# Layer 0's first stage: single k tiles, three a_u heads, and an order of three engines written out

## The chip, the cores and the metric

The kernel runs on one core of a Trainium2 chip. The metric is the device time of one execution in microseconds (us). Engines are named as in the profile: PE (TensorE), with PEld for its weight loads, DVE (VectorE), ACT (ScalarE), POOL (GpSimd) and SP (SyncE, which only issues DMAs here; its queue is SPq).

## The reference

Two trunk layers work on a latent stream x (256 x 2048) and a context stream ctx (256 x 2048), in float32. What matters for the change is the start of layer 0:

```python
shift, scale, gate = split(silu(c) @ w_mod[l] + b_mod[l], 3)
h   = rmsnorm(x, g_pre[l]) * (1 + scale) + shift          # the same for ctx with c_ctx
proj = h @ w_in[l]
a_u, a_v, a_g, b_q, b_k, b_v, b_g, c_x, c_g = split_cols(proj)
y_a = chunk_gmlp(gelu(a_u), gelu(a_v), ...) * silu(a_g)   # a_u, a_v: 512 columns, 4 heads of 128
...
x = x + gate * rmsnorm(concat(y_a, y_b, y_c) @ w_out[l], g_post[l])
```

So nothing of layer 0 can be multiplied before shift and scale of at least one slice of 128 features are known, and they need columns of w_mod (2048 x 6144 per layer), and 1/rms of every token, which needs all of x.

## The kernel before

**Tiling.** The 2048 features are 16 k tiles of 128 (KT). Both streams lie side by side, feature-major, as 16 tiles yo0..yo15 of 128 x 512 (256 latent and 256 context tokens). Every product with w_in is done as three passes (mm3, L383): hi x hi, hi x lo, lo x hi, with each operand cut exactly into two float32r parts. h becomes hh and hl per k tile (make_h, L445: two DVE operations, two ACT casts and two DVE operations of 128 x 256). Weights come as halves of 128 x 1024 (512 KB) into one of three raw buffers; ACT casts whi (L367) and DVE subtracts wlo (L368). Stream (L329) hands them out in a fixed order.

**The first stage of layer 0** (layer, L496) runs over k outermost and keeps six sums in PSUM, four of a_v (128 tokens x 512 columns each) and two of a_u (heads 0 and 1, "au01"). For each k it does 12 products of a_v (start_av) and 6 of a_u (start_au). The two other a_u heads follow as units of their own (tunit, L473: one head of 128 columns, 16 k tiles x 3 passes = 48 products), then c_x, a_g, c_g, k, v, q, b_g, and the output projection.

**The modulation** of k tiles k0.. (mod_start, L154) is computed inside this stage on PE: silu(c) (cpad, 32 columns wide) against scale and shift columns of w_mod, in four groups kg of four k slices. DVE transposes the sum (L177), eight tiny products gather it (ps_modc, L182), and DVE adds biases to get gs and sh (L191 to L194, "the columns"). It comes by pairs of k tiles for k 0 to 7 (PAIRS; 4 MB of w_mod per pair, 16 DMAs of 256 KB into the hh8..hl15 tiles) and by single tiles for k 8 to 15 (ALONE; 2 MB per tile, into two sets of buffers taken in turn). mod_start is a generator: the loop over blocks steps the next block's products between the a_v and a_u products of this one.

**Order.** PE's order is the program's (manual_schedule). The other engines' orders are found by the tile framework, which orders instructions by priority and by their data. The remaining modulation (gate of layer 0, all of layer 1; mod_rest, L265) runs on DVE as multiply-adds of 128 x 512 (L209), so many steps per weight half by RATE and pace (L287). Later (L296) hands other engines' products back to PE after delays counted in PE time; branch_a yields such delays before the mixing products (ps_mix). NEAR (L279) says how many weight halves ahead of the one in use are requested at the start.

**Buffers.** PSUM has six "mm" banks (the sums of products) and two "ms" banks for small things (ps_mod, ps_modc, ps_rs, ps_rb, ps_mix). w2k is a ring of seven 2 KB-per-partition tiles.

**The start** (L989 to L1014): the small loads, x in 16 DMAs, sums of squares (ACT L467, DVE L468), first modulation block, 1/rms (col_sums, POOL pow, bcast as ps_rb), two weight halves, then layer(0).

Of the kernel before, what the change touches and what calls it, by code (L numbers as in the profile page):

```python
# [23 lines left out]
PAIRS, ALONE = [0, 2, 4, 6], list(range(8, KT))  # L24
# [3 lines left out]
def units():  # L28
    """(name, first column, columns, first k tile, k tiles): blocks of w_in of 128 x 2048 each."""
    u = []  # L30
    u += [("av", COL["av"], 512, 4 * i, 4) for i in range(4)]
    u += [("au01", COL["au"], 256, 8 * i, 8) for i in range(2)]
    u += [(f"au{h}", COL["au"] + 128 * h, 128, 0, 16) for h in (2, 3)]
    u += [(f"cx{h}", COL["cx"] + 128 * h, 128, 0, 16) for h in range(4)]
    u += [(f"ag{h}", COL["ag"] + 128 * h, 128, 0, 16) for h in range(4)]
    u += [(f"cg{h}", COL["cg"] + 128 * h, 128, 0, 16) for h in range(4)]
    u += [(f"k{h}", COL["k"] + 128 * h, 128, 0, 16) for h in range(2)]
    u += [("v", COL["v"], 256, 8 * i, 8) for i in range(2)]
    u += [(f"q{h}", COL["q"] + 128 * h, 128, 0, 16) for h in range(8)]
    u += [(f"bg{h}", COL["bg"] + 128 * h, 128, 0, 16) for h in range(8)]  # L40
    return u
# [25 lines left out]
def trunk_kernel(ctx: ExitStack, tc: tile.TileContext, xT, xhalf, cT, wss, wsl, wmod, win, wout0, wout1, const, vec, rows,  # L67
# [24 lines left out]
    # ---- constants  # L92
    ct = sb([P, KT, 2], F32, "ct")
    DMA.dma_start(ct, cT)
    vecs = sb([P, 2, NVEC], F32, "vecs")
    DMA.dma_start(vecs, vec)
# [8 lines left out]
    A.activation(cs, ct, AF.Silu)  # L105
    cpad = sb([P, KT, 32], F32, "kt0")
    V.memset(cpad, 0.0)
    V.tensor_copy(cpad[:, :, 0:2], cs)

    class low:  # L110
        """instructions that may wait for the next `n`."""
# [22 lines left out]
    # ---- modulation: columns [128, 16, stream] of scale, shift and gate  # L134
# [5 lines left out]
    def mod_cols(l, cb, ps8):  # L140
        """ps8 [128, 4, 2]: silu(c) @ w_mod for 512 columns of column block cb."""
        what, j0 = cb // 4, (cb % 4) * 4
        b = vc(l, "bmod")[:, cb * 4:cb * 4 + 4].unsqueeze(2).to_broadcast([P, 4, 2])
        sl = slice(j0, j0 + 4)
        if what == 0:
            V.tensor_tensor(out=sh[l][:, sl], in0=ps8, in1=b, op=ALU.add)
        else:
            dst = (gs[l] if what == 1 else gg0)[:, sl]
            g = vc(l, "gpre" if what == 1 else "gpost")[:, sl].unsqueeze(2).to_broadcast([P, 4, 2])
            V.scalar_tensor_tensor(out=dst, in0=ps8, scalar=1.0 if what == 1 else 0.0, in1=b,  # L150
                                   op0=ALU.add, op1=ALU.add)
            V.tensor_tensor(out=dst, in0=dst, in1=g, op=ALU.mult)

    def mod_start(k0, nk):  # L154
        """scale and shift of k tiles k0 .. k0 + nk - 1 of layer 0 on the tensor engine: yields after
        each unit's products, and before the columns."""
        ps = ms_ps("mod")
        n = 2 * P * nk
        for kg in range(4):
            src = wss[PAIRS.index(k0), kg] if nk == 2 else wsl[ALONE.index(k0), kg]  # L160
            if nk == 1:
                tags = (("mraw", "mraw", "macc", "vv"), ("mg", "mgl", "yo0 yo1", "yo2 yo3"))[k0 % 2][kg]
            else:
                tags = " ".join(f"{t}{8 + 2 * kg + i}" for i in range(2) for t in ("hh", "hl"))
# [31 lines left out]
    def mod_dve(l, cb, red):  # L196
        """red [128, 2, 16]: sums over the 32 partitions of each quadrant, transposed."""
# [38 lines left out]
    def mod_gate1():  # L236
        """products of silu(c) and the gate's columns of w_mod in layer 1, still to be summed over partitions."""
# [16 lines left out]
    def gate1():  # L254
        """(sum + b_mod) * g_post of layer 1's gate, on all partitions."""
        for c in range(4):
            r = sb([P, 2, 512], F32, "mraw", 2)
            DMA.dma_start(r, rows[None, :, c * 512:(c + 1) * 512].to_broadcast([P, 2, 512]))
            ps = ms_ps("gate")
            PE.matmul(ps, ones, g1[c], start=True, stop=True)  # L260
            V.tensor_tensor(out=g1[c], in0=r[:, 0], in1=ps, op=ALU.add)
            V.tensor_tensor(out=g1[c], in0=g1[c], in1=r[:, 1], op=ALU.mult)
            yield YT
# [13 lines left out]
    RATE = dict(au0=2, cx0=2.2, ag0=2.2, cg0=2.2, k0=2, v0=2, q0=1.8, bg0=2.2, out0=2.8,  # L277
                k1=2.5, v1=2.5, q1=1, bg1=2.2)
    NEAR = [1] * 6 + [0] * 6 + [1, 2, 3]  # L279
# [7 lines left out]
    def pace():  # L287
        """steps of the modulation due per half of a unit, behind the latest weights on the vector engine."""
# [6 lines left out]
    # ---- work of other engines that hands products back to the tensor engine later  # L295
    class Later:  # L296
# [19 lines left out]
        def flush(self):  # L316
# [8 lines left out]
            (("yo8 yo9", 1), ("yo10 yo11", 1)), (("yo12 yo13", 1), ("yo14 yo15", 1))]  # L325
    BACK = 8

    # ---- weights: raw -> exact parts hi + lo, in halves of a unit, ahead of their use
    class Stream:  # L329
        AHEAD = 3  # L330

        def __init__(self):
            self.src, self.out, self.pos, self.stop = [], [], 0, 0
            self.place, self.behind = {}, {}
            for l in range(2):
                def half(name, i, h):
                    return win[l, UIDX[name][i], h]
                for i in range(2):
                    self.src += [half("av", 2 * i, 0), half("au01", i, 0), half("av", 2 * i, 1),
                                 half("av", 2 * i + 1, 0), half("au01", i, 1), half("av", 2 * i + 1, 1)]  # L340
                for i, u in enumerate(UNITS):
                    if u[0] not in ("av", "au01"):
                        self.src += [win[l, i, 0], win[l, i, 1]]
# [10 lines left out]

        def emit(self):
            tags = self.place.get(len(self.out), (("whi", NHI), ("wlo", NLO)))
            r = sb([P, 1024], F32, "raw", NRAW)
            DMA.dma_start(r, self.src[len(self.out)])
# [29 lines left out]
    def part(w, c):  # L388
        """columns c of both parts; a part is a tile or a list of tiles side by side."""
# [19 lines left out]
    # ---- per-token reciprocal rms from sums over features  # L409
# [14 lines left out]
    def col_sums(ps, q, n, start=True, stop=True):  # L424
        """columns of ps: sums over the partitions of q [128, n * 128], one accumulation group."""
# [10 lines left out]
    # ---- streams in feature-major tiles  # L436
    yo = [None] * KT
# [7 lines left out]
    def make_h(l, k, rb, streams):  # L445
        """h = x * rstd * gs + sh, as hi + lo; rb: rstd over the tokens of `streams`."""
# [26 lines left out]
    def tunit(n, sl=None):  # L473
        """feature-major product of one unit of 128 columns: PSUM [128, n]."""
# [18 lines left out]
    blocks = [(k, 2) for k in PAIRS] + [(k, 1) for k in ALONE]  # L493

    # ---- one layer, up to the inputs of the output projection
    def layer(l):  # L496
# [12 lines left out]
        # a_v (token-major) and two heads of a_u, k outermost  # L509
        av = [mm_ps("av") for _ in range(nt)]  # L510
        au = [mm_ps("au") for _ in range(2)]
# [6 lines left out]
        def start_au(k):  # L518
            for j in range(2):
                c = slice((k % 4) * 256 + j * P, (k % 4) * 256 + (j + 1) * P)  # L520
                mm3(au[j][:, 0:n], part(auw, c), (hh[k][:, 0:n], hl[k][:, 0:n]), k == 0, k == KT - 1)
            later.tick(PASS * 512 * nt + PASS * n * 2)

        for i, (k0, nk) in enumerate(blocks):
            mod = mod_start(*blocks[i + 1]) if l == 0 and i + 1 < len(blocks) else iter(())

            def step():
                next(mod, None)

            for k in range(k0, k0 + nk):  # L530
                made = prep_h(l, k)
            if l == 1 and i == 0:
# [7 lines left out]
            for _ in range(2 if nk == 2 else 4):  # L540
                step()
            start_av(k0, range(nt))
            if nk == 2:
                start_au(k0)
                step()
                step()
                start_av(k0 + 1, range(nt // 2))
            step()
            if nk == 2:
                start_av(k0 + 1, range(nt // 2, nt))  # L550
# [28 lines left out]
        # branch A  # L579
        def branch_a():  # L580
            vt = [w2k([P, 512]) for _ in range(nt)]
            ss = sb([P, 4], F32, "ss")
            for j in range(2):
# [8 lines left out]
            yield 12.0 if l == 0 else 7.0  # L592
            for h in range(4):
# [9 lines left out]
                yield (12.0 if h == 1 else 2.0) if l == 0 else (7.0 if h == 1 else 2.0)  # L603

        # branch C
# [9 lines left out]
        def fourier(g, ps):  # L615
            """cos(2 pi t m / 256) is even in t around 128 and sin odd: positions t and 256 - t are added for the one
            and subtracted for the other, which leaves 128 rows each (position 128 in the sines' row of t = 0)."""
# [25 lines left out]
        # branch B  # L643
        def rope(hi, lo, ps):
            """x * cos + rot(x) * sin of the latents, and x of the context, as hi + lo."""
# [97 lines left out]
        for h in (2, 3):  # L743
# [56 lines left out]
    # ---- output projection  # L800
# [33 lines left out]
    def finish():  # L834
        """layer 1's output projection with tokens on partitions, and x1 + gate * y / rms(y)."""
        x1 = {}

        def turn():
            """x1 of the latents to tokens on partitions: [128, token tile, 512] per 512 columns."""
# [68 lines left out]
    def boundary(s, acc):  # L908
        """x1 = x0 + gate * y / rms(y) of stream s in place, and its own 1 / rms."""
# [50 lines left out]
    def prep_h(l, k):  # L960
        new_h(k)
        if l == 0:
            return make_h(0, k, rb0, [0, 1])
        return make_h(1, k, rbs[0], [0])

# [23 lines left out]
    with tc.manual_schedule(engines={mybir.EngineType.PE}):  # L989
        # ---- start: modulation of the first k tiles, x and its statistics  # L990
        raw = w2k([P, NFIRST])
        DMA.dma_start(raw, const[:, 0:NFIRST])
        A.copy(identr, raw[:, 0:P])
        A.copy(cst[:, 0:NFIRST - P], raw[:, P:])
        for k in range(KT):
            yo[k] = sb([P, T], F32, f"yo{k}")
            DMA.dma_start(yo[k], xT[k])
# [3 lines left out]
        m = mod_start(*blocks[0])  # L1001
# [3 lines left out]
        dg = rstd_diag(ps[:, 0:4], 4, D)  # L1005
# [4 lines left out]
        next(m)  # L1010
        W.emit()
        W.emit()
        list(m)
# [81 lines left out]
```

## Time and profile before

| what | value |
|---|---|
| median of 3 runs | 1171.07 us (1170.23 to 1173.67) |
| profiled execution: span from the first to the last instruction | 1167.9 us |
| mean granted TensorE clock | 0.996 |
| PE matmul groups of units (ps_t, L384 to L386) | 1346.5 us of records, which overlap, 3888 products |
| HBM read | 231.08 MB, 200 GB/s over the span |
| DMA, 10 to 120 us | 338 to 398 GB/s |
| first a_v product / last of the stage | 37.30 us / 136.4 us |
| DVE after the stage, waiting before wlo at 141.67 | 5.64 us |

The profiled execution's own device time isn't listed apart from its span; the median of the runs is 3.2 us above the span. A row of the timeline or of the chain begins with its start and its length in us; matmul records overlap, since they are pipelined, so the distance between starts (0.23 us for a product of 512 columns) is the cost of one.

### The profile page before, as it was taken

The numbers are of one execution on the slowest core, as the hardware profiler recorded it, in microseconds if no ns is written. First come the engines' busy times: TensorE is split into PE (matmuls) and PEld (weight loads), VectorE is DVE, ScalarE is ACT, GpSimd is POOL, SyncE is SP. The second block draws the span as 40 slices with busy tenths as digits, with TensorE's granted clock in tenths as the row PEclk, the third lists the DMA queues.
The fourth block names the chain that finished last, engine by engine and source line by source line (L and its number), as shares of the span: only waits on it lengthen the run. The fifth ranks groups of instructions, "written<-read, shape, count | busy, mean of one in ns | idle before, by whom it ended". The sixth has DMA issues, their size and how long they took to land.

```text
span 1167.9 us, 17483 instructions
## 1 busy us (share of the span) xinstructions
PE 1136.0 (97%) x6656; PEld 953.7 (82%) x6656; DVE 881.8 (76%) x1469; ACT 509.8 (44%) x914; POOL 17.3 (1%) x23
## 2 busy tenths in 40 slices
PE   3999999999999999999999999999999999999996
PEld 1466688888898888888888888889899999997885
DVE  5454498888988878798989886495896678888554
ACT  4222513322224667632533233365563278745442
POOL 0000000000000000000000000200000000000001
PEclk9999999999999999999999999999999999999998
DMA  9999765466665334455466665365656665688563
GB/s 339 378 387 357 254 196 166 145 202 193 200 200 178 105 114 136 134 175 173 158 199 209 205 216 162 109 207 173 205 158 205 203 200 178 195 269 244 190 187 120
DMA packets 73892, 234.32 MB, mean 201 GB/s; under 512 B 8528, under 2 KB 9680, under 8 KB 73808
## 3 DMA queue, kind: packets, MB, share of 16 engines
q1 hardware_dynamic: 73808, 233.21, 61.6%
q8 instruction: 52, 0.85, 0.3%
q14 instruction: 32, 0.26, 0.1%
HBM read 231.08 MB, written 2.10 MB: 200 GB/s over the span
## 4 chain that ended last, share of the span: by engine, by line
PE 92%; DVE 3%; DMA 2%; ACT 2%; issue 1%; POOL 0%; SPq 0%; DVEq 0%; ACTq 0%; POOLq 0%
PE ps_t L384 20%; PE ps_t L385 20%; PE ps_t L386 20%; PE ps_mod L172 3%; PE ps_av L384 2%; PE ps_y L386 2%; PE ps_y L384 2%; PE ps_y L385 2%; PE ps_av L385 2%; PE ps_av L386 2%; PE ps_v L386 1%; PE ps_v L384 1%; PE ps_v L385 1%; PE ps_tp L722 1%; PE ps_au L384 1%
## 5 line engine op out<-in xcount | busy, mean ns | idle before, releaser
L384 PE MATMUL ps_t<-hh,whi 128*128 128x512 f32 (+1 forms) x1296 | 452.1, 349 | 0.0
L386 PE MATMUL ps_t<-hh,wlo 128*128 128x512 f32 (+1 forms) x1296 | 447.4, 345 | 0.0
L385 PE MATMUL ps_t<-hl,whi 128*128 128x512 f32 (+1 forms) x1296 | 447.0, 345 | 0.0
L367 ACT CAST whi<-raw 128x1024 fp32r<-128x1024 f32 x218 | 228.2, 1050 | 397.3 <-PE ps_t L385 274.4
L368 DVE TENSOR_TENSOR wlo<-raw,whi 128x1024 fp32r<-128x1024 f32 x218 | 265.3, 1220 | 99.1 <-ACT whi L367 98.8
L384 PEld LDWEIGHTS ps_t<-hh,whi 128*128 128x128 f32 x1296 | 244.9, 189 | 34.3 <-issue 4.6
L386 PEld LDWEIGHTS ps_t<-hh,wlo 128*128 128x128 f32 x1296 | 244.7, 189 | 30.6
L385 PEld LDWEIGHTS ps_t<-hl,whi 128*128 128x128 f32 x1296 | 244.9, 189 | 28.9 <-issue 0.5
L209 DVE SCALAR_TENSOR_TENSOR macc<-mraw,cs,macc 128x512 f32<-128x512 f32 x360 | 249.9, 745 | 17.6 <-DMA mraw<-in_wmod_dram 17.5
L455 ACT ACTIVATE hh<-w2k,sh 128x256 fp32r<-128x256 f32 x64 | 29.0, 502 | 61.4 <-DVE w2k L451 61.4
L384 PE MATMUL ps_y<-whi,hh 128*128 128x512 f32 x112 | 45.0, 401 | 0.0
L386 PE MATMUL ps_y<-whi,hl 128*128 128x512 f32 x112 | 43.8, 392 | 0.0
L385 PE MATMUL ps_y<-wlo,hh 128*128 128x512 f32 x112 | 43.7, 390 | 0.0
L384 PE MATMUL ps_av<-whi,hh 128*128 128x512 f32 x96 | 40.0, 416 | 0.0
L385 PE MATMUL ps_av<-wlo,hh 128*128 128x512 f32 x96 | 37.9, 395 | 0.4 <-DVE wlo L368 0.4
L172 PE MATMUL ps_mod<-hh,kt 128*32 128x512 f32 x64 | 21.5, 649 | 17.0 <-DMA hh<-in_wss_dram 17.0
L386 PE MATMUL ps_av<-whi,hl 128*128 128x512 f32 x96 | 37.6, 392 | 0.0
L386 PE MATMUL ps_v<-whi,hl 128*128 128x256 f32 x128 | 36.2, 283 | 0.0
L384 PE MATMUL ps_v<-whi,hh 128*128 128x256 f32 x128 | 36.2, 283 | 0.0
L385 PE MATMUL ps_v<-wlo,hh 128*128 128x256 f32 x128 | 36.2, 283 | 0.0
L468 DVE TENSOR_TENSOR acc<-acc,w2k 128x512 f32<-128x512 f32 (+1 forms) x33 | 21.2, 641 | 18.7 <-ACT w2k L467 17.2
L401 ACT CAST w2k<-ps_tp 128x512 fp32r<-128x512 f32 x40 | 23.5, 587 | 22.8 <-PE ps_scc L385 12.0
(292 smaller groups left out, 1491.8 us busy)
## 6 DMA issues: line engine op xcount, KB each, us to landing
raw<-in_win_dram SPq DMA_DIRECT2D x160, 512.0 KB, 4.1
mraw<-in_wmod_dram SPq DMA_DIRECT2D x128, 512.0 KB, 4.3
raw<-in_wout_dram SPq DMA_DIRECT2D x64, 512.0 KB, 4.2
hh<-in_wss_dram SPq DMA_DIRECT2D x32, 256.0 KB, 5.6
hl<-in_wss_dram SPq DMA_DIRECT2D x32, 256.0 KB, 5.4
yo<-in_xT_dram SPq DMA_DIRECT2D x16, 256.0 KB, 5.4
mraw<-in_wsl_dram SPq DMA_DIRECT2D x8, 512.0 KB, 6.9
yo<-in_wsl_dram SPq DMA_DIRECT2D x16, 256.0 KB, 7.2
```

Of the source, the lines that this page charges most:

```text
L172: PE.matmul(ps[32 * kk:32 * kk + 32, 0:n], cpad[:, kg * 4 + kk], ws[kk], start=kg == 0, stop=kg == 3, tile_position=(0, 32 * kk))
L209: V.scalar_tensor_tensor(out=acc[:, s], in0=w[:, kk % 2], scalar=c, in1=acc[:, s], op0=ALU.mult, op1=ALU.add)
L367: A.copy(ph, r[:, c])
L368: self.last = V.tensor_tensor(out=pl, in0=r[:, c], in1=ph.bitcast(F32), op=ALU.subtract)
L384: PE.matmul(ps, st[0], mv[0], start=start, stop=False)
L385: PE.matmul(ps, st[0], mv[1], start=False, stop=False)
L386: PE.matmul(ps, st[1], mv[0], start=False, stop=stop)
L401: A.copy(hi, src)
L455: first = A.activation(hh[k][:, sl], t[:, sl], AF.Identity, bias=sh[l][:, k, s:s + 1])
L468: V.tensor_tensor(out=acc[:, sl], in0=acc[:, sl], in1=q[:, sl], op=ALU.add)
L722: PE.transpose(tp[:, (2 * j + b) * P:(2 * j + b + 1) * P], src, ident)
```

## The change

In layer 0's first stage all modulation comes by single k tiles, the loop runs k by k, and a third a_u head is summed along with the other two, in an "ms" bank; its weights are taken from the stream in the stage, and its unit behind the stage goes. Layer 1 keeps its pairs. DVE, ACT and SP take the program's order from the first load to the end of the stage (first_stage), with the weight loads and splits at k tiles given by two lists. The start is reordered: x before the constants, Silu inside the written order, the first modulation is that of k 0 alone, three weight halves are split ahead. Odd k tiles below 8 keep part of their modulation weights in hh14 to hl15, and the third head's weights lie in hh12 to hl13 and, later, yo4 to yo7. Delays of branch_a and one rate are set anew.

```diff
-PAIRS, ALONE = [0, 2, 4, 6], list(range(8, KT))
+PAIRS, ALONE = [0], list(range(KT))
...
+    yo = [sb([P, T], F32, f"yo{k}") for k in range(KT)]
     ct = sb([P, KT, 2], F32, "ct")
-    DMA.dma_start(ct, cT)
     vecs = sb([P, 2, NVEC], F32, "vecs")
-    DMA.dma_start(vecs, vec)
...
-    A.activation(cs, ct, AF.Silu)
     cpad = sb([P, KT, 32], F32, "kt0")
     V.memset(cpad, 0.0)
-    V.tensor_copy(cpad[:, :, 0:2], cs)
...
             if nk == 1:
-                tags = (("mraw", "mraw", "macc", "vv"), ("mg", "mgl", "yo0 yo1", "yo2 yo3"))[k0 % 2][kg]
+                odd = ("hh14 hl14", "hh15 hl15") if k0 < 8 else ("yo0 yo1", "yo2 yo3")
+                tags = (("mraw", "mraw", "macc", "vv"), ("mg", "mgl") + odd)[k0 % 2][kg]
...
-    RATE = dict(au0=2, cx0=2.2, ag0=2.2, cg0=2.2, k0=2, v0=2, q0=1.8, bg0=2.2, out0=2.8,
+    RATE = dict(au0=2, cx0=2.2, ag0=2.2, cg0=2.2, k0=2, v0=2, q0=1.8, bg0=2.2, out0=3.0,
                 k1=2.5, v1=2.5, q1=1, bg1=2.2)
-    NEAR = [1] * 6 + [0] * 6 + [1, 2, 3]
+    NEAR = [0] * 14 + [1, 2, 3]
+    LOADS = [0, 1, 2, 4, 5, 6, 6, 8, 9, 10, 12, 13, 14]
+    SPLITS = [1, 2, 3, 5, 6, 7, 7, 9, 10, 11, 13, 14, 15]
...
+    AU2 = [(("hh12 hl12", 1), ("hh13 hl13", 1)), (("yo4 yo5", 1), ("yo6 yo7", 1))]
...
                 for i in range(2):
-                    self.src += [half("av", 2 * i, 0), half("au01", i, 0), half("av", 2 * i, 1),
+                    third = [half("au2", 0, i)] if l == 0 else []
+                    if l == 0:
+                        self.place[len(self.src) + 2] = AU2[i]
+                    self.src += [half("av", 2 * i, 0), half("au01", i, 0), *third, half("av", 2 * i, 1),
                                  half("av", 2 * i + 1, 0), half("au01", i, 1), half("av", 2 * i + 1, 1)]
...
+        def load(self):
+            r = sb([P, 1024], F32, "raw", NRAW)
+            DMA.dma_start(r, self.src[len(self.raws)])
+            self.raws.append(r)
+
         def emit(self):
+            if len(self.raws) == len(self.out):
+                self.load()
+            r = self.raws[len(self.out)]
             tags = self.place.get(len(self.out), (("whi", NHI), ("wlo", NLO)))
-            r = sb([P, 1024], F32, "raw", NRAW)
-            DMA.dma_start(r, self.src[len(self.out)])
...
-        au = [mm_ps("au") for _ in range(2)]
+        au = [mm_ps("au") for _ in range(2)] + [ms_ps("au") for _ in range(1 - l)]
...
+            if l == 0:
+                mm3(au[2], part(au2w, slice((k % 8) * P, (k % 8 + 1) * P)), (hh[k], hl[k]), k == 0, k == KT - 1)
...
+        if l == 0:
+            for k in range(KT):
+                new_h(k)
+                make_h(0, k, rb0, [0, 1])
+                m = mod_start(k + 1, 1) if k + 1 < KT else iter([None] * 4)
+                for _ in range(4):
+                    next(m)
+                for _ in range(LOADS.count(k)):
+                    W.load()
+                for _ in range(SPLITS.count(k)):
+                    W.emit()
+                if k % 2 == 0:
+                    avw = W.next()
+                if k % 4 == 0:
+                    auw = W.next()
+                if k % 8 == 0:
+                    au2w = W.next()
+                start_av(k, range(nt))
+                list(m)
+                start_au(k)
+            first_stage.close()
...
-            yield 12.0 if l == 0 else 7.0
+            yield 9.0 if l == 0 else 7.0
...
-                yield (12.0 if h == 1 else 2.0) if l == 0 else (7.0 if h == 1 else 2.0)
+                yield (4.0 if h == 1 else 2.0) if l == 0 else (7.0 if h == 1 else 2.0)
...
-        for h in (2, 3):
+        for h in range(len(au), 4):
             ps = tunit(n)
...
+    EN = mybir.EngineType
+    first_stage = ExitStack()
+    with tc.manual_schedule(engines={EN.PE}):
+        first_stage.enter_context(tc.manual_schedule(engines={EN.DVE, EN.Activation, EN.SP}))
+        DMA.dma_start(ct, cT)
+        for k in range(KT):
+            DMA.dma_start(yo[k], xT[k])
         raw = w2k([P, NFIRST])
         DMA.dma_start(raw, const[:, 0:NFIRST])
+        DMA.dma_start(vecs, vec)
+        A.activation(cs, ct, AF.Silu)
+        V.tensor_copy(cpad[:, :, 0:2], cs)
         acc0 = sb([P, T], F32, "acc")
         for k in range(KT):
             add_sq(acc0, yo[k], FULL, k == 0)
-        m = mod_start(*blocks[0])
+        A.copy(identr, raw[:, 0:P])
+        A.copy(cst[:, 0:NFIRST - P], raw[:, P:])
+        W.load()
+        m = mod_start(0, 1)
         next(m)
         ps = ms_ps("rs")
         col_sums(ps, acc0, 4)
-        dg = rstd_diag(ps[:, 0:4], 4, D)
+        r0 = rstd_cols(ps[:, 0:4], 4, D)
+        W.emit()
+        dg = w2k([P, 4, P])
+        for j in range(4):
+            V.tensor_scalar(out=dg[:, j], in0=ident, scalar1=r0[:, j:j + 1], scalar2=None, op0=ALU.mult)
+        next(m)
+        next(m)
         next(m)
         rb = bcast(dg, 4)
         rb0 = w2k([P, T])
         V.tensor_copy(rb0, rb)
-        next(m)
+        W.load()
+        W.load()
+        list(m)
         W.emit()
         W.emit()
-        list(m)
         layer(0)
```

More of the change, by code (lines that the diff above doesn't have):

```diff
@@ L333, in __init__ @@
             self.src, self.out, self.pos, self.stop = [], [], 0, 0
+            self.raws = []
             self.place, self.behind = {}, {}
@@ L338, in __init__ @@
                 for i in range(2):
-                    self.src += [half("av", 2 * i, 0), half("au01", i, 0), half("av", 2 * i, 1),
+                    third = [half("au2", 0, i)] if l == 0 else []
+                    if l == 0:
+                        self.place[len(self.src) + 2] = AU2[i]
+                    self.src += [half("av", 2 * i, 0), half("au01", i, 0), *third, half("av", 2 * i, 1),
                                  half("av", 2 * i + 1, 0), half("au01", i, 1), half("av", 2 * i + 1, 1)]
                 for i, u in enumerate(UNITS):
-                    if u[0] not in ("av", "au01"):
+                    if u[0] not in ("av", "au01") + ("au2",) * (l == 0):
                         self.src += [win[l, i, 0], win[l, i, 1]]
@@ L434, in bcast @@
         return ps
-    yo = [None] * KT
     hh = [None] * KT
@@ L491, in hold_unit @@
         return ps
-    blocks = [(k, 2) for k in PAIRS] + [(k, 1) for k in ALONE]
+    blocks = [(k, 2) for k in range(0, 8, 2)] + [(k, 1) for k in range(8, KT)]
     def layer(l):
@@ L521, in start_au @@
                 mm3(au[j][:, 0:n], part(auw, c), (hh[k][:, 0:n], hl[k][:, 0:n]), k == 0, k == KT - 1)
+            if l == 0:
+                mm3(au[2], part(au2w, slice((k % 8) * P, (k % 8 + 1) * P)), (hh[k], hl[k]), k == 0, k == KT - 1)
             later.tick(PASS * 512 * nt + PASS * n * 2)
[L524 to L528, printed above, removed]
+        if l == 0:
[19 more added lines that the diff above has]
+            first_stage.close()
+        for i, (k0, nk) in enumerate(blocks if l else ()):
             for k in range(k0, k0 + nk):
-                made = prep_h(l, k)
-            if l == 1 and i == 0:
+                new_h(k)
+                made = make_h(1, k, rbs[0], [0])
+            if i == 0:
                 W.behind = {len(W.out): made, len(W.out) + 1: made}
@@ L539, in layer @@
                 auw = W.next()
-            for _ in range(2 if nk == 2 else 4):
-                step()
             start_av(k0, range(nt))
@@ L544, in layer @@
                 start_au(k0)
[L545 to L550, printed above, removed]
+                start_av(k0 + 1, range(nt))
             start_au(k0 + nk - 1)
@@ L582, in branch_a @@
             ss = sb([P, 4], F32, "ss")
-            for j in range(2):
+            for j in range(len(au)):
                 A.activation(ytmp(j), au[j][:, 0:n], AF.Gelu_apprx_tanh)
@@ L958, in boundary @@
         rbs[s] = r
[L960 to L964, printed above, removed]
     def after_start(l):
@@ L987, in boundary_ctx @@
                 yield YH
-    with tc.manual_schedule(engines={mybir.EngineType.PE}):
+    EN = mybir.EngineType
[5 more added lines that the diff above has]
+            DMA.dma_start(yo[k], xT[k])
         raw = w2k([P, NFIRST])
         DMA.dma_start(raw, const[:, 0:NFIRST])
[L993 to L997, printed above, removed]
+        DMA.dma_start(vecs, vec)
+        A.activation(cs, ct, AF.Silu)
+        V.tensor_copy(cpad[:, :, 0:2], cs)
         acc0 = sb([P, T], F32, "acc")
```

## The prediction, as it was put on record

> **What bounds the kernel now.** I read the page's busy rows and its 40 slices first, then the start in stretches of 10 us, then the chain of waits there, then single instructions.
>
> ```profile
> span 1167.9 us, 17483 instructions
> PE 1136.0 (97%) x6656; PEld 953.7 (82%) x6656; DVE 881.8 (76%) x1469; ACT 509.8 (44%) x914; POOL 17.3 (1%) x23
> PE   3999999999999999999999999999999999999996
> DMA  9999765466665334455466665365656665688563
> ```
>
> TensorE (PE) is busy in all slices but the first (29 us) and the last. The DMA engines are full only in the first four. So time can be won only where PE starts, and anything lost behind PE's back elsewhere must first become a wait of PE. The start in stretches (columns: length; busy PE, PEld, DVE, ACT, POOL; granted clock; DMA share; GB/s):
>
> ```profile
> 10.00:20.00 10.00, 2.98 (x8) 0.72 (x8) 8.03 (x12) 6.34 (x11) 0.00 (x0) 1.00 1.05 390
> 20.00:30.00 10.00, 8.63 (x37) 2.78 (x36) 4.00 (x8) 2.09 (x2) 1.03 (x1) 0.83 1.04 396
> 30.00:40.00 10.00, 9.10 (x38) 3.46 (x37) 5.47 (x13) 2.75 (x5) 0.00 (x0) 1.00 1.05 386
> ```
>
> DMA sits at its ceiling, 386 to 396 GB/s; PE's "busy" here is mostly waiting inside matmul records. The chain of waits (start, length, what):
>
> ```profile
> 6.01 5.43 DMA yo<-in_xT_dram
> 11.46 5.42 DMA hh<-in_wss_dram
> ...
> 24.50 2.04 PE ps_rb L433 x2
> 26.54 4.14 PE ps_mod L172 x16
> ...
> 31.82 5.56 PE ps_mod L172 x16
> 37.37 0.43 PE ps_av L384
> ...
> 41.70 2.83 PE ps_mod L172 x16
> 44.53 0.43 PE ps_av L384
> ```
>
> The first a_v product stands at 37.4, behind the whole first pair of modulation columns (last tile used at 29.6) and half of the second (31.8 to 37.4: 5.56 us for 16 records that take 1.86 when nothing is awaited). The second k tile's a_v starts at 44.5. From there PE runs densely, as in the single-k part:
>
> ```profile
> 99.53 1.86 PE ps_mod L172 x32
> 101.39 0.43 PE ps_av L384
> ...
> 104.31 0.18 PE ps_modc L182 x8
> 104.49 0.43 PE ps_au L384
> ...
> 106.08 1.86 PE ps_mod L172 x32
> 107.94 0.43 PE ps_av L384
> ```
>
> One k tile costs 107.94 - 101.39 = 6.55 us (6.58 for its neighbours; I use 6.58): mod 1.86, 18 products at 0.23, and the switches.
>
> **The change, part by part. First products earlier.** In tiles of 256 KB, which land every 0.68 us here, the old order has 36 tiles ahead of 29.6: 16 of x, 16 of the first pair, 4 of weights. The new first a_v waits for x (16), mod of k 0 (8), mod of k 1 (8) and three weight halves (6): 38 tiles, +1.4 us. x is issued at 1.18 instead of 2.12 (-0.94), as the two small loads (81 and 88 KB, 0.44 us at 390 GB/s) go behind it. Last tile: 29.6 + 1.4 - 0.94 + 0.44 = 30.5; its products 0.4: a_v at about 31.0.
>
> **The other chain to that point** is VectorE's, in its written order. Mod of k 0 has landed 12 tiles (8.2 us) before 30.5, at 22.3. Then: products 0.9 (at the slow rate seen at 26.5), broadcast of 1/rms 2.04, its copy 0.69, columns 0.45, two weight splits 2.35 that stand ahead of h, and t, hh, hl of one tile 1.94: 30.7. The two ends meet. From below a_v can't pass 30.5; from above I take 33, if the splits wait for their casts as well (two of 1.04). I take 31.0. The moved Silu, identity and constants copies lie under the loads of x.
>
> **The cadence.** au2 adds three products of 0.23 per k tile: 6.58 + 0.69 = 7.27 us. Loads per k tile: 8 tiles of mod, 1.75 of weights on average, 9.75 x 0.68 = 6.6 us, so PE sets the pace. a_v of k 1 is at 31.0 + 7.27 = 38.3; a_v of k 15 follows 13 x 7.27 + (4.74 + 0.69) = 99.9 later, at 138.2 (4.74 is the old distance from k 14 to 15, with no mod inside, 127.61 to 132.35); the last tile takes 4.44 + 0.69 = 5.13 (old: 132.35 to 136.79). **The au3 unit starts at 143.3.** Before, au2's own unit starts at 136.79 and au3's at 149.61, with the four mg products (1.72) inside. They move into au3's unit unchanged, so the like point is 147.9. **Gain: 147.9 - 143.3 = 4.5 us.** It nets three things: a_v of k 1 6.2 us earlier, but one more mod still to do (1.9), and the paired part, at 6.4 a tile, now pays the single tile's switches.
>
> **New waits.** The third a_u sum holds one of two "ms" PSUM buffers, so mod of k+2 can't start before VectorE has read the columns of k+1. Those take 0.45 us after modc, a_u of that k takes 2.1: hidden, 1.6 to spare. h of k+1 needs 2.4 us from modc's end (124.24 to 126.63), under 2.1 + 1.9 of a_u and mod: 1.6 to spare as well. A weight split (cast 1.05, then 1.22) stands between transpose and columns on VectorE, under a_v's 2.9; in k 7 there are two, which may cost 0.2. I take 0 for these; the worst, all split-bearing tiles late by half a microsecond, would be 6. On SyncE's queue a weight load waits for the split three back, and all later mod loads stand behind it; by the lists that split is at least one k tile old, mostly two, and loads run up to two tiles ahead. Cost 0 with that cover; without it, see the last rival.
>
> **Behind the stage.** With au2's unit gone, one unit instead of two covers the gelus, squares, scalings and the weights of cx0. Before, the split of cx0's first half ends at 149.9 (the one starting 148.70), 13.1 us after 136.79; now it must be there 11.1 + 1.7 = 12.8 after. Two casts and two splits (4.5 us in all on both engines) have left that spell, one gelu (0.64) joins it. The mixing products come at 9 instead of 12, about 11.5 us in with mg; their input was ready at 10.2 and is now at 10.8. I take 0, up to 3. Two modulation steps (4 x 0.745 each) move from this spell to later ones, and out0 does 3.0 per unit instead of 2.8; VectorE has 1 us in 10 free there, and PE waited nowhere in it: 0, up to 2. Layer 1's loop keeps its order.
>
> **Sum.** Span 1167.9 - 4.5 = 1163.4. The median of the runs, 1171.07, lies 3.2 above that profiled span; I keep the 3.2: **1166.6**. About 0.3% (3.5 us) is what can be told from no change here.
>
> **Rivals.** (a) A slow clock at the first a_v. The granted clock after PE stood idle from 23.1 to 24.5 was:
>
> ```profile
> 25.00:26.00 1.00, 1.00 (x2) 0.00 (x0) 0.00 (x0) 0.39 (x1) 0.00 (x0) 0.50 0.98 389
> 26.00:27.00 1.00, 1.00 (x5) 0.20 (x8) 0.42 (x1) 0.76 (x2) 0.00 (x0) 0.50 1.04 389
> ```
>
> It was half for some 3 us. The new start is thinner: 0.46 us of products per 1.36 us of loading, against two thirds before, and before, the clock was full at 37.4. Three microseconds of a_v at half rate lose 1.5: 1168.1. [...]
>
> (b) The cover behind the stage is too thin: PE waits for cx0's weights or the mixing. Against it: VectorE idled 5.6 us in that spell before. With the 3 us of above: 1169.6.
>
> (c) Slower: the hand-written load queue becomes the bound. A SyncE wait for a split or for a mod buffer holds every load behind it, and DMA runs dry, as it did in single-k stretches (355 and 357 GB/s at 108 to 114 and 121 to 128, 338 at 80 to 100). A k tile's 2.56 MB need 7.27 us at 352 GB/s, so below that the loads decide; at 337 the gain is gone (7.59, 14 tiles), below 327 the kernel is over 0.3% slower. At 320: 8.0 a tile, +10 - 4.5: 1176.6. Against it: those stretches were paced by PE at 6.58, not by the queue.
>
> (d) Better: loads let a_v start at 30 (-1.0), and au3's unit, whose buffer the first gelu frees, no longer waits for it, since that sum now ends two heads before the stage does (-0.4, the gap before 136.79): 1165.2.
>
> **How the numbers follow.** Forecast 0.55, (a) 0.12, (b) 0.09, (c) 0.13, (d) 0.11. The forecast's own spread, 1166.1 (a_v at 30.5) to 1168.6 (at 33), lies mostly below 1167.6; with (d) and a part of (a): faster by over 0.3%: 0.58. Most of (a) and (b), the upper end of the forecast and a little of (c): within 0.3%: 0.30. Slower: 0.12, from (c). The range reaches from 1164.0, below (d) by what the unpriced waits could give back, to 1172.0, over (b) and the 2 us of out0; what is left out is most of (c).
>
> **What would show it.** In the profile after: the first a_v product at 30.5 to 33 (was 37.4) with the granted clock at 1.00 in that stretch; a_v starts 7.2 to 7.4 apart; DMA under full share from about k 3 on; no waits of PE for modc or mod buffers; the au3 unit at 143 to 144 and no hole before cx0's. Wrong if the distance is above 7.5, if SyncE's mod loads start later than two tiles ahead, or if PE waits for whi or wlo behind the stage.

## The result, and the profile after

The changed kernel takes 1176.02 us (median of 12 runs, 1174.21 to 1179.26); the kernel before took 1171.82 (12 runs, 1170.23 to 1175.76) beside it. The ratio is 1.0037, with a 95% interval of 1.0025 to 1.0049: 4.2 us slower. Forecast were 1166.6 us, at most 1172.0, with 0.12 on slower. The forecast was wrong in sign.

Every run's time is its span plus 1.8 us. So the profiled execution before, with a span of 1167.9, stood for 1169.7, which is 2.1 below the median of 1171.82, and the one after, 1176.4, for 1178.2, which is 2.2 above its own. The two profiles differ by 8.5 us, the medians by 4.2; about half of what the two profiles show as lost is thus the spread between executions, and only the experiments size the losses.

The busy row and the slice row of PE of the kernel after (span 1176.4 us):

```profile
PE 1133.0 (96%) x6816; PEld 960.8 (82%) x6816; DVE 884.8 (75%) x1487; ACT 508.1 (43%) x916; POOL 18.0 (2%) x23
PE   3999999999999999999999998999999999997996
```

PE is busy for 3 us less than before in a span 8.5 us longer. The first slice is still 3; where all others but the last had 9, the slices from 706 and from 1059 us now have 8 and 7. The DMA engines are full from 10 to 40 us as before (a share of 1.03 to 1.05 in both; 400, 403 and 405 GB/s in stretches of 10 us; 390, 396 and 386 before). The chain of waits at the start and inside the stage (start, length, what):

```profile
28.04 3.64 PE ps_mod L170 x32
31.68 0.76 PE ps_av L395
...
37.85 1.86 PE ps_mod L170 x32
39.71 0.43 PE ps_av L395
...
104.97 0.43 PE ps_av L395
...
112.23 0.43 PE ps_av L395
```

The first a_v product moved from 37.4 to 31.7, the second k tile's from 44.5 to 39.7, and k tiles are 112.23 - 104.97 = 7.26 us apart. The stage does what was forecast; its end comes 2.6 us earlier than at the like point before (au3's unit at 145.28 against 147.89, which is its 149.61 less the 1.72 of the mg products), and 2.4 of that is still there at the first product of v (326.9 against 329.3). So the time is lost later. PE's waits from 700 to 760 us (the first two lines) and from 1040 to 1160 (the rest), after (us in all, times, longest):

```profile
PE ps_t L397 <- DVE mraw L379: 3.1, 1, 3.1
PE ps_t L395 <- ACT mraw L378: 0.9, 1, 0.9
...
PE ps_y L397 <- DVE hl L821: 2.2, 1, 2.2
PE ps_x L870 <- DVE nstrh L259: 1.9, 1, 1.9
PE ps_x L870 <- DVE ctrh L259: 1.8, 1, 1.8
```

Before, the first window has neither wait, and the second only these two:

```profile
PE ps_x L847 <- DVE ctrh L261: 0.7, 1, 0.7
PE ps_x L847 <- DVE nstrh L261: 0.4, 1, 0.4
```

Two places, then: the last units of layer 0, and the start of layer 1's output projection.

**The first place.** The last weights of layer 0 are split ahead into mraw, macc and mg, the buffers of the remaining modulation, and can only go there when its last column block has been transposed. VectorE's timeline there, after (start, length, engine, line, what):

```profile
714.67 1.29 DVE L213 STREAM_TRANSPOSE mraw<-macc 128x512 f32<-128x512 f32 x2
...
718.22 1.22 DVE L379 TENSOR_TENSOR mraw<-raw,mraw 128x1024 fp32r<-128x1024 f32 x1
```

and before:

```profile
706.44 0.70 DVE L215 STREAM_TRANSPOSE mraw<-macc 128x512 f32<-128x512 f32 x1
...
710.88 1.22 DVE L368 TENSOR_TENSOR mraw<-raw,mraw 128x1024 fp32r<-128x1024 f32 x1
```

The chain of multiply-adds ends 8 us later although PE is 2 us earlier, and the split that PE needs starts at 718.22 instead of 710.88. **The second place** looks alike: the last multiply-adds of layer 1's gate sum (nstrl) end at 1067.1 instead of 1058.3, and hl, ctrh and nstrh stand behind them on VectorE. Of these 8.8 us, 3.2 are inherited: PE itself is that much later here (last products of ps_o at 1044.5 against 1041.3).

### The profile page after: what moved, and what is told of

The parts are those of the page before. It is cut to its first block, busy times and chain, and to the rows that moved or that the text cites. A ratio compares the mean times of both kernels' runs of the same rounds, so it can differ in the third digit from the quotient of the medians.

```text
span 1176.4 us, 17789 instructions
## 1 busy us (share of the span) xinstructions
PE 1133.0 (96%) x6816; PEld 960.8 (82%) x6816; DVE 884.8 (75%) x1487; ACT 508.1 (43%) x916; POOL 18.0 (2%) x23
## 4 chain that ended last, share of the span: by engine, by line
PE 70%; DVE 14%; DMA 10%; issue 3%; ACT 3%; SPq 0%; POOL 0%; DVEq 0%; ACTq 0%; POOLq 0%
PE ps_t L395 13%; PE ps_t L397 13%; PE ps_t L396 13%; DMA mraw<-in_wmod_dram 7%; DVE macc L207 5%; DVE wlo L379 3%; PE ps_mod L170 3%; PE ps_av L395 2%; PE ps_y L395 2%; PE ps_y L397 2%; PE ps_y L396 2%; PE ps_av L396 2%; PE ps_av L397 2%; PE ps_au L395 1%; PE ps_v L397 1%
## 5 line engine op out<-in xcount | busy, mean ns | idle before, releaser
L395 PE MATMUL ps_t<-hh,whi 128*128 128x512 f32 (+1 forms) x1280 | 445.8, 348 | 1.0 <-ACT yo L607 1.0
L397 PE MATMUL ps_t<-hh,wlo 128*128 128x512 f32 (+1 forms) x1280 | 440.7, 344 | 0.0
L396 PE MATMUL ps_t<-hl,whi 128*128 128x512 f32 (+1 forms) x1280 | 440.6, 344 | 0.0
L378 ACT CAST whi<-raw 128x1024 fp32r<-128x1024 f32 x216 | 225.8, 1048 | 377.9 <-PE ps_t L396 249.5
L395 PEld LDWEIGHTS ps_t<-hh,whi 128*128 128x128 f32 x1280 | 242.2, 189 | 34.3 <-issue 4.6
L397 PEld LDWEIGHTS ps_t<-hh,wlo 128*128 128x128 f32 x1280 | 242.2, 189 | 29.5
L396 PEld LDWEIGHTS ps_t<-hl,whi 128*128 128x128 f32 x1280 | 242.3, 189 | 27.5 <-issue 0.5
L395 PE MATMUL ps_av<-whi,hh 128*128 128x512 f32 x96 | 39.7, 413 | 0.0
L468 DVE SCALAR_TENSOR_TENSOR hl<-w2k,sh,hh 128x256 fp32r<-128x256 f32 x64 | 28.5, 481 | 3.2 <-ACT hh L465 3.2
```

The costliest lines, as they stand in the source:

```text
L378: A.copy(ph, r[:, c])
L395: PE.matmul(ps, st[0], mv[0], start=start, stop=False)
L396: PE.matmul(ps, st[0], mv[1], start=False, stop=False)
L397: PE.matmul(ps, st[1], mv[0], start=False, stop=stop)
L468: last = V.scalar_tensor_tensor(out=hl[k][:, sl], in0=t[:, sl], scalar=sh[l][:, k, s:s + 1], in1=hh[k][:, sl].bitcast(F32), op0=ALU.add, o ...
```

## The experiments

The theory after this reading: both losses are the background work of RATE being late, not the first stage. (1) With au2's unit gone the phase au0 has one unit instead of two, so two modulation steps fewer are issued there; out0 at 3.0 instead of 2.8 was to make up for them. (2) The steps that are left over as a fraction after layer 0 (state["owed"]) are 0.4 of a step instead of 0.8, so layer 1's gate steps pass the next whole number one weight half later in places (its step 32, by counting the program's steps, at half 76 instead of 75). The rival theory: the losses come from elsewhere in the changed stage. The first four kernels ran on one chip with the kernel before at 1171.07; the next four on another at 1171.22, the last three at 1171.39. In the text, "+" and "-" are differences of medians to that; the ratios given beside them compare executions taken together and can differ from the quotient of the medians by some 0.1%.

**steps_both**: after, with both made good: the one unit behind the stage takes the four steps of the former two, and out0 goes back to 2.8.

```diff
-    RATE = dict(au0=2, cx0=2.2, ..., out0=3.0,
+    RATE = dict(au0=4, cx0=2.2, ..., out0=2.8,
```

> The changed kernel with the rates of the kernel before from c_x on: the single unit left behind the stage takes all four modulation steps (au0 = 4) and out0 goes back to 2.8, so that every step from c_x on, and the fraction left over for layer 1, stand where they stood before. Theory 1 (the modulation on VectorE runs two steps behind and is paced by VectorE and its loads, so it hands mraw and macc over late to the last weights of layer 0, and the gate's sums late to layer 1's output projection): the waits of PE for mraw (0.9 and 3.1 us in the changed kernel's profile) go, those for hl, ctrh and nstrh fall to what they were before (about 1 us), and the gain of the stage comes through: 1168 to 1170.5. Theory 2 (the 11 us of the removed unit were the time in which VectorE did that work, and no schedule gives them back): still 1173 or more, with the waits for mraw.

Measured: 1168.29 us, ratio 0.9977 (0.9965 to 0.9988): -2.8. VectorE's timeline:

```profile
702.52 0.70 DVE L213 STREAM_TRANSPOSE mraw<-macc 128x512 f32<-128x512 f32 x1
```

Twelve microseconds earlier than after, and PE's wait for mraw is gone. With two numbers of the schedule set anew the kernel is faster than before: the stage was a gain all along. The second place did not go as expected: the wait for hl is gone, but PE still waits 3.5 for ctrh and 1.0 for nstrh, where about 1 in all was expected. This execution is 2.1 above its kernel's median, and warm's (below), with the same steps, has 1.6 and 0.9. So the waits of a single execution size the second place to no better than 2 us; the medians do.

**steps_mod**: the two steps alone; the fraction stays at the change's value.

```diff
-    RATE = dict(au0=2, cx0=2.2, ..., out0=3.0,
+    RATE = dict(au0=4, cx0=2.2, ..., out0=3.0,
```

> The changed kernel with au0 = 4 alone; out0 stays at 3.0, so the fraction left over for layer 1 stays 0.4 and the last step of layer 1's gate is issued one weight half later than before. Theory 1: the waits for mraw at 715 to 720 us go, those at the start of layer 1's output projection stay: 1171 to 1173. Theory 2: as the changed kernel, 1175 to 1177.

Measured: 1171.36 us, ratio 1.0001 (0.9992 to 1.0010): +0.3. The waits for mraw are gone, and layer 1's wait of 2.2 for hl stays. The last multiply-adds of the gate, first in steps_both, then here:

```profile
1056.61 0.74 DVE L245 SCALAR_TENSOR_TENSOR nstrl<-mraw,cs,nstrl 128x512 f32<-128x512 f32 x1
...
1059.23 1.54 DVE L245 SCALAR_TENSOR_TENSOR nstrl<-mraw,cs,nstrl 128x512 f32<-128x512 f32 x2 [1.02 <-DMA mraw<-in_wmod_dram]
```

They end 3.4 us later here, although PE begins layer 1's output projection at the same time in both (1059.89 and 1059.66): the gate is late by the fraction alone. The chain's last transposes stand at 702.93 and 705.85, as with out0 at 2.8 (702.52 and 705.45): the rate of out0 doesn't move the chain's end.

**tail_only**: the fraction alone; the steps stay late.

```diff
         W.stop = 0
+        state["owed"] += 0.4
         later.flush()
```

> The changed kernel with 0.4 added to the left-over fraction at the end of layer 0, so that layer 1's gate steps stand where they stood before, and nothing else. If the one weight half is what makes the gate late, the waits for hl, ctrh and nstrh (5.9 us in the profile) fall to about 1 and the time to 1172 to 1173.5, with the waits for mraw kept. If the gate is late because layer 0 ends late, nothing changes: 1175 to 1177.

Measured: 1173.13 us, ratio 1.0021 (1.0007 to 1.0035): +2.1. Now layer 1's wait for hl is gone, and the first place is as in the kernel after, with waits of 3.1 and 1.6 for the two parts of mraw.

The four make a square, with the +4.2 taken from the result above. From +4.2 the two steps give back 4.2 - 0.3 = 3.9 us alone, and 2.1 + 2.8 = 4.9 when the fraction is right; the fraction gives 2.1 alone and 3.1 beside the steps; both give 7.0. Each such figure is uncertain by about 2 us.

**before_late**: the kernel before, with only these two losses put in.

```diff
-    RATE = dict(au0=2, cx0=2.2, ..., out0=2.8,
+    RATE = dict(au0=1, cx0=2.2, ..., out0=3.0,
```

> The kernel before with the step rates of the change alone: au0 = 1, so that two steps fewer are done by c_x, and out0 = 3.0. Theory 1: PE waits for mraw in the held units and for the gate's sums as in the changed kernel, and the time rises by what it lost behind the stage: 1175 to 1180. Theory 2: with both units behind the stage VectorE has its time, and the kernel stays at 1171 to 1172.5.

Measured: 1178.30 us, ratio 1.0062 (1.0050 to 1.0075): +7.2, with waits of 3.1 for mraw, 1.7 for hl and 1.8 for ctrh. PE reaches the held units when it did before (their first product is at 717.55 in both), and the split that it needs starts at 719.73 instead of 710.88. The old stage with the new schedule loses what the new stage loses, 7.0. The rival theory falls.

**before_frac**: the kernel before with the smaller fraction alone (state["owed"] -= 0.4 in the place of tail_only's line).

> The kernel before with 0.4 taken off the left-over fraction at the end of layer 0 (0.8 becomes 0.4, as in the changed kernel) and nothing else. If the fraction sets the place of the last gate step, PE waits for hl by about 2 us at the start of layer 1's output projection and the time rises by 2.5 to 3.5 us, to 1173.5 to 1174.5; else 1171.

Measured: 1172.71 us, ratio 1.0012 (1.0003 to 1.0021): +1.5, with the wait for hl (1.8) and 1.9 for ctrh. The mechanism is there, its price is under what was expected and under the 2.1 to 3.1 of the square. Its size is thus known as 1.5 to 3 us, no better.

**warm**: steps_both with products on PE that nobody reads (fp32, 128 x 512, into a free "mm" bank), 15 ahead of the first modulation product and one after each of its first three groups.

```diff
         W.load()
+        wps = mm_ps("warm")
+        def warm(n):
+            for _ in range(n):
+                PE.matmul(wps, ones, cpad.rearrange("p a b -> p (a b)"), start=True, stop=True)
+        warm(15)
         m = mod_start(0, 1)
```

> steps_both with idle-time products on PE that nobody reads: 15 of 128x512 ahead of the first modulation product, and one behind each of its first three groups, so that PE isn't at half rate at the start. Theory A (the start lost to the forecast because PE ran at half rate from 18.6 to 33 us: mod of k 1 took 3.64 us for 1.86, the first a_v products 0.43 for 0.23): a_v of k 0 at about 30.3 instead of 31.7, a_v of k 1 at about 37.8 instead of 39.6, and 1.5 to 2 us less than steps_both, 1166.3 to 1167. Theory B (loads or VectorE's chain set that point): a_v of k 1 stays at 39 to 39.7 and the time at 1168.3.

Measured: 1168.22 us, ratio 0.9974 (0.9963 to 0.9985): -3.0, not to be told from steps_both. PE did run at the full rate (a broadcast of 1/rms 1.13 us, 2.04 in the kernel after), but the first a_v, at 31.19, waited 0.75 for hh, and the fill products stood in the way of the real ones (the last group of k 0 at 25.10; 23.57 in the kernel after). The second k tile's a_v is at 38.51: 1.1 earlier than after, but 1.0 later than in steps_both's own profile, where PE had found the full rate by itself. The expected gain was missed: behind the slow products, VectorE's chain and the loads end within about a microsecond.

**tail_early**: steps_both with layer 1's gate steps issued earlier (k1 and v1 from 2.5 to 3.0; by counting, the last step falls at half 74 instead of 75, and those during q1 up to four halves earlier).

> steps_both with k1 = v1 = 3.0 instead of 2.5, so that layer 1's gate steps end two weight halves sooner. If the gate's lateness still costs PE what its profile shows there (3.5 for ctrh, 1.0 for nstrh), 1164 to 1167; if those waits come from the loads of rows behind the last steps and from hl, not from the steps, 1168.3 as steps_both.

Measured: 1172.16 us, ratio 1.0004 (0.9995 to 1.0013): +0.9, so 3.7 worse than steps_both. ctrh is waited for only 0.2 us, but hh 1.5, hl 0.6 and nstrh 1.9. Steps that come too early cost as well.

**two_heads**: single k tiles and the order written out, as in the change, but two a_u heads; au2's unit, branch_a's delays and out0's 2.8 are those of before.

```diff
-        au = [mm_ps("au") for _ in range(2)] + [ms_ps("au") for _ in range(1 - l)]
+        au = [mm_ps("au") for _ in range(2)]
...
-    LOADS = [0, 1, 2, 4, 5, 6, 6, 8, 9, 10, 12, 13, 14]
-    SPLITS = [1, 2, 3, 5, 6, 7, 7, 9, 10, 11, 13, 14, 15]
+    LOADS = [1, 2, 3, 5, 6, 6, 8, 9, 10, 12, 13]
+    SPLITS = [2, 3, 5, 6, 7, 9, 10, 11, 13, 14, 15]
```

> The single k tiles and the written order alone: two a_u heads in the stage, au2's own unit back behind it, weight lists shifted to match, rates and delays of the kernel before (au0 = 2 over two units, so the same steps). If the gain of the stage is that of the single first tile, a_v of k 1 stands at about 39, tiles are 6.58 apart, and the time is that of steps_both, 1167.5 to 1169. If the third head is what gains (its cover for h, or PSUM), 1171 to 1172.

Measured: 1167.77 us, ratio 0.9962 (0.9949 to 0.9975): -3.5. As expected for a gain of the single first tile, the second a_v is at 39.3 and tiles are 6.58 apart. With two heads au0 has its two units and four steps by itself, and nothing is late: no wait for mraw, 0.2 for hl. Two waits of the three-head forms are gone too: 1.0 at au3's unit (below), and those for w2k in ps_f, 2.1 in steps_both and 1.1 in warm. There four steps lie in one unit's time instead of two; but branch_a's delays differ as well and were not varied alone, so the cause of these two waits is not separated.

**two_heads_again, two_heads_frac, three_frac**: whether the gate steps are still too late now that the start is earlier. The first repeats two_heads; the others add tail_only's line to two_heads and to steps_both.

> The two-head form once more, as the control for the next two kernels on their chip. Expected 1167.0 to 1168.5 us with the kernel before at 1171.2, and PE waiting about 2.4 us for ctrh and 1.4 for nstrh at the start of layer 1's output projection.

> Two heads, with 0.4 of a step added to the fraction that layer 0 leaves over, so that layer 1's gate steps come one weight half earlier where the fraction decides. Theory: with the start about 3 us earlier, what now ends last is layer 1's gate chain on VectorE, which did not move along (PE waits 3.8 us for ctrh and nstrh, 1.1 in the kernel before); earlier steps take 1 to 2 us off these waits and off the time: 1165.5 to 1167. Rival: an earlier step only meets the splits and h's of the units ahead, as with k1 and v1 at 3.0; then waits for hh or hl appear and the time is the control's or up to 2 us above.

> Three heads with au0 at 4 and out0 at 2.8, and the same 0.4 added to the fraction. Theory: as for the two-head form, 1 to 2 us off the waits for ctrh (3.5) and nstrh (1.0): 1166.5 to 1167.5, and about 0.5 to 1 us above the two-head form, since the waits of ps_f for w2k (2.1 us at 136 to 330) stay. Rival: new waits for hh or hl, 1168 to 1171. If three heads come out over 0.5 us below two, the third head is worth something after all.

Measured: 1166.14 (ratio 0.9960, 0.9944 to 0.9975), 1168.23 (0.9974, 0.9965 to 0.9984) and 1170.77 us (1.0002, 0.9993 to 1.0012). The theory of these three missed; the rival has the times, but mostly not the waits (0.6 for hl, with three heads): PE's waits for w2k in ps_o rose from 1.7 to 2.8 us with two heads, and from 1.5 in steps_both to 3.2 with three. The line also does something else than was expected. By counting, it makes the fraction 1.2, and so a whole step: the first gate step falls at the first weight half of layer 1 instead of half 40, 15 others fall one half earlier, and the last stays at half 75. The traces agree: with two heads the first operation on ctrh starts at 848.9 instead of 889.4, the last on nstrl at 1055.9 against 1055.1. So 0.4 of a step less, which puts the last step and 19 others one half later, costs 1.5 to 3.1 us. 0.4 more costs 2.1 (two heads, same chip) to 2.5 (three, another chip), but leaves the last step where it was: whether a last step one half earlier would pay isn't shown by these runs. On the same chip and with the line, three heads stand 2.5 us above two; without it, -2.8 stands against -3.5 and -5.3, a difference of 0.7 to 2.5. The third head thus brings nothing that these runs show, and two_heads, 3.5 and 5.3 us below the kernel before in two batches, is the best form that was run.

## Why the prediction was wrong

**First products: right.** Forecast 31.0 (30.5 to 33) for the first a_v: 31.65 in the kernel after. In steps_both it is at 30.27, so "can't pass 30.5" was 0.2 too strict. Both ends that the forecast saw meeting, loads and VectorE's chain, do meet, as warm shows.

**Rival (a), the slow clock: it happened, in part.** Forecast 38.3 for the second a_v, measured 39.71. The broadcast of 1/rms took 2.04 us where it takes 1.12 in steps_both, the first eight modulation products from mg 1.08 against 0.64, and the first three a_v products 0.76, 0.43 and 0.43, where later they take 0.43, 0.23 and 0.23. (That all 32 modulation products before the first a_v took 3.64 us, and those before the second 1.86, is no such sign: in steps_both the former took 3.63 at the full rate, waiting for loads.) The granted clock in these rows reads 1.00 throughout, so the sign that the forecast had named, a clock of 1.00, says nothing here; the durations and the distances between starts do. The two rates show here, and that they vary between executions: steps_both is at the full rate from 24.74 on, the kernel after not before about 33, although PE had products there from 18.63 on with idle times of 0.56 us at most. What changes the rate isn't shown by these runs. Its price was put at 1.5 us. Here 39.71 - 38.3 = 1.4, half of it from the later first a_v and half from the slow a_v products. Of five profiled executions with three heads (warm and tail_early left out), two have the second a_v at 39.2 and 39.6 with slow products before it (first a_v 0.80 us long), and three at 37.6 to 37.9 (0.50): 1.2 to 2.1 us. There was no net gain when the slow rate was removed in warm.

**The cadence: right.** 7.27 forecast, 7.26 measured, so the new waits cost nothing, as forecast. **Rival (c)**, the load queue as the bound, gave 1176.6 and the time came out at 1176.02, but its mechanism isn't there: DMA ran at 392 GB/s from 80 to 100 us and at 334 and 251 in the next two stretches of 20 us, and no wait of PE is listed from 39 to 136 us. The number was met by chance.

**The au3 unit: 143.3 forecast, 145.28 measured.** 1.4 of the 2.0 is the late second a_v above. 1.0 is a wait where rival (d) saw a gain of 0.4. ScalarE's and PE's timeline after:

```profile
142.27 1.05 ACT L378 CAST whi<-raw 128x1024 fp32r<-128x1024 f32 x1 [2.29 <-issue]
143.34 1.28 ACT L607 ACT_TABLE_LOAD   x1
144.63 1.57 ACT L607 ACTIVATE yo<-ps_au 128x512 f32<-128x512 f32 x3
145.28 0.50 PE L395 MATMUL ps_t<-hh,whi 128*128 128x512 f32 x1 [1.03 <-ACT yo L607]
```

The au sum is done early, but on ScalarE's queue the gelu that frees its bank stands behind a weight cast, before which ScalarE was idle for 2.29 us without a cause that the profile shows, and a table load. The same 1.03 is in steps_both; two_heads doesn't have it. The remaining -0.4 lies in the stage behind the second k tile, which is that much shorter than counted.

**Behind the stage: the step that failed.** It read: "Two modulation steps (4 x 0.745 each) move from this spell to later ones, and out0 does 3.0 per unit instead of 2.8; VectorE has 1 us in 10 free there, and PE waited nowhere in it: 0, up to 2." It priced the steps as work, 6 us to be fitted somewhere, and looked for a lack of room. What counts is lateness. The steps are a chain with a due time, and the spells that follow issue 2.2 steps per unit of 48 x 0.23 = 11 us, so being two steps short means being 10 us behind (714.67 against 702.52 in steps_both, 12.2, while PE reaches ps_o at the same time in both, 388.5 and 388.7). out0's higher rate should have made that up, and by counting it does (the chain's last step falls at the 19th weight half of out0 before and after); but the chain takes 35 to 36 us per column block at 3.0 and at 2.8 alike (678.70 to 714.67 after, 670.84 to 706.44 before). VectorE's idle times in it end with the chain's own loads (0.2 to 1.7 us each), but for one of 0.26 behind a weight cast, so these and VectorE's work look like its pace; no run tests that. Measured: 3.9 to 4.9 us. That "PE waited nowhere in it" before showed a margin without its size: the split into mraw ended at 712.1 before, and this is the product that needs it:

```profile
717.78 0.28 PE L386 MATMUL ps_t<-hh,mraw 128*128 128x256 f32 x1
```

A margin of 5.7 us, then. After, the split is 7.3 us later, and PE would have been there 2.3 us sooner, an estimate: at 719.5 less its waits of 0.9 and 3.1. 7.3 + 2.3 - 5.7 = 3.9, and the two waits make 4.0.

**"Layer 1's loop keeps its order": wrong.** The program of layer 1 is the same, but the fraction of a step that it inherits is not, and one weight half's difference cost 1.5 to 3.1 us at the far end of the kernel.

**Sum.** Stage, with its clock and its wait: -2.8 (steps_both) instead of -4.5. Steps and fraction together: +7.0 instead of 0. Measured: +4.2.

## What to carry to other kernels

Work that is paced by counts (so many steps per unit) moves when a unit is removed or a rate is rounded anew: count for each such chain at which place in the program each step falls before and after, up to the last consumer, and price its lateness against the wait that ends last there, not its duration. Free time on an engine does not by itself bring a late chain forward: here a rate of 3.0 instead of 2.8 left it at 35 to 36 us per column block. And when a restructured stage comes out slower, put the schedule's constants right one by one before giving up the restructuring: here the stage was worth 3 us, and two constants hid it.

## What the hardware showed unasked

- The granted clock of the profile's rows can read 1.00 while products take about twice their time: the broadcast of 1/rms took 2.04 us in the kernel after and 1.12 in steps_both, and the reading is 1.00 in both. The kernel before has the same 2.04 with a reading of 0.50 (24.5 to 27.5 us).
- Whether the first products run at about half rate varies between executions of nearly the same kernel. Of nine profiled executions with the change's start (warm left out), six had the first a_v at 31.3 to 31.7 us, with a record 0.79 to 0.80 long, and three had it at 30.3 to 30.6, with 0.50. The broadcast took 2.04 to 2.05 us in five of the six (not read in tail_early), and 1.12 and 1.13 in two of the three (not read in three_frac).
